# Three FFN down projections: eight of 22 inputs folded into seven block products, in written order

## The chip, the core and the metric

The kernel runs on one core of a Trainium2 chip, as one launch. The metric is device time in microseconds, the median of several runs. The engines are TensorE (PE; its weight loads are PEld), VectorE (DVE), ScalarE (ACT), GpSimd (POOL) and SyncE (SP). SP, ACT and POOL have DMA queues of their own.

## What is computed

An encoder of two layers on 512 tokens of width 1024. Each layer has an FFN, an attention mixer and a second FFN, so there are four FFNs:

```python
def swiglu(h, w_gate, w_up, w_down):
    return (jax.nn.silu(h @ w_gate) * (h @ w_up)) @ w_down
...
        h = rms_norm(x, norm_g[l, 0])
        x = x + 0.5 * swiglu(h, ffn_w_gate[l, 0], ffn_w_up[l, 0], ffn_w_down[l, 0])
```

The inner width is 2816, or 22 blocks of 128; the outer width is 8 blocks of 128. All data is float32. The change touches the last matrix product, `@ w_down`, in the first three FFNs. The fourth has a different ending (`finish`), which also forms the output.

## The kernel before

**Arithmetic.** A float32 factor is written as a high and a low part of type fp32r. A product of two factors is then three matmuls: high by high, high by low, low by high. ScalarE makes a high part by a cast and VectorE the low part by a subtraction. `weights` (L90 to L99) loads a weight tile on SP into `raw`, casts it to `whi` (L96) and subtracts to `wlo` (L97). `parted` (L101 to L106) does the same for a tile that is there already. There are three buffers of `raw` and four each of `whi` and `wlo`, so the fifth cast waits until TensorE is done with the first.

**Tokens** are the moving operand: 512 columns, cut into halves of 256 (`H`) where blocks are formed.

**Gate and up.** A tile `m` (one of the 22 inner blocks) is made by `Seven.tile`. Gate and up weights, with two groups of four inputs, form a 2 x 2 block product which is computed with seven products in place of eight, in the order 1, 5, 6, 2, 7, 3, 4. Sums of weights (`wsum`, `others`) and sums of inputs (`Sides`) are formed beforehand. A product is "joined" (`wide`) where the high and low halves of an input stand side by side as one 512 column operand, so each high weight is used by one matmul of 512 columns in place of two of 256. `Seven.in_order` ties the instructions of a tile on each engine to the order in which they are written; elsewhere a scheduler picks the order. Product 4 of a tile and its gating are put off into the next tile (`self.tail`). At the end of a tile `g`, the gated value, is split into `hi` and `lo`.

**Down.** For each of 8 output blocks, loop over the 22 inputs in chunks of 8, 8 and 6; per input three matmuls of 512 columns (L379, L380 and L382), 66 in an output block, all into one PSUM bank. Then `advance` adds the result to the residual: VectorE scales (L284) and adds (L285); POOL stores the new residual and loads the next (`x_keep`, `x_tile`); ScalarE makes the high part of the next norm's input with its gain (L149) and the square (L160); VectorE makes the low part (L150) and sums the squares (L161). The scheduler orders this stage. The tail of the last gate and up tile (`tiles.flush`) stands behind the first chunk of the first output block.

**Copies for later FFNs.** `ahead_by` issues, in paces, DMAs that form sums of the next FFN's gate and up weights in DRAM (`d_odd`, `d_even`), from ACT's and POOL's queues.

Of the kernel before, what the change touches and what calls it, by code (L numbers as in the profile page):

```python
# [11 lines left out]
F32 = mybir.dt.float32  # L12
# [19 lines left out]
GBUFS = 2 * MF  # L32
# [11 lines left out]
def encoder(ctx: ExitStack, tc: tile.TileContext, a: dict, out: bass.AP):  # L44
# [41 lines left out]
    loaded, lower, kept = [], [], []  # L86
    prepared, ahead, due, owed, queue = {}, [], [], [0.0, 0.0], {}
# [45 lines left out]
    class Norm:  # L133


        def __init__(self, step, gain):
            self.step, self.gain = step, gain
            self.hi, self.lo, self.both = [None] * KC, [None] * KC, [None] * KC
            self.acc = None
# [5 lines left out]
        def parts(self, k, xk):  # L145
            g = self.gain[:, k : k + 1]
            both = self.both[k] = xpool.tile([P, 2, S], F32R, tag=f"h{k}", name=f"h{k}")
            hi, lo = both[:, 0], both[:, 1]
            nc.scalar.activation(hi, xk, AF.Copy, scale=g)  # L149
            nc.vector.scalar_tensor_tensor(out=lo, in0=xk, scalar=g, in1=f(hi), op0=ALU.mult, op1=ALU.subtract)  # L150
            self.hi[k], self.lo[k] = hi, lo

# [53 lines left out]
    def table_loads(fp):  # L206
        nc.gpsimd.memset(tab, 0.0)
        hot.extend(fp.tile([64, 512], F32R, tag="g", name="hot", bufs=GBUFS) for _ in range(2))
        for r in (0, 32):
            nc.gpsimd.dma_start(tab[r : r + 32, 0:8], a["rel_bias_table"][:, 4:12])  # L210
            nc.gpsimd.dma_start(tab[r : r + 32, 32:36], a["rel_bias_table"][:, 0:4])
        for i in range(2):
            nc.gpsimd.dma_start(hot[i], a["one_hot"][:, i * 512 : (i + 1) * 512])

    def position_tables(fp):


        parts = fp.tile([64, 36], F32R, tag="g", name="parts", bufs=GBUFS)
        nc.scalar.copy(parts, tab)
        nc.vector.tensor_tensor(out=parts[32:64], in0=tab[32:64], in1=f(parts[32:64]), op=ALU.subtract)  # L220
        yield
        for i in range(2):
            ps = st_tile()
            nc.tensor.matmul(ps[0:36, :], parts, hot[i], start=True, stop=True)
            td = fp.tile([36, 512], F32, tag="g", name="td", bufs=GBUFS)
# [15 lines left out]
    def small_loads(fp):  # L241
        nc.gpsimd.dma_start(mask, a["na_mask"])
        for l in range(DEPTH):
# [6 lines left out]
            lq = fp.tile([P, 2, 2, 64], F32, tag="g", name="lq", bufs=GBUFS)  # L250
# [5 lines left out]
    def lambda_sums(fp, l):  # L256
        lq = own[l][3]
        lp = fp.tile([P, 2, 64], F32, tag="g", name="lp", bufs=GBUFS)
# [20 lines left out]
    def advance(m, ps, rb, fp, nxt):  # L279

        t = x_tile(m)
        room = quarters(fp)
        d, sq = [room[:, n : n + 2, :].rearrange("p a c -> p (a c)") for n in (0, 2)]
        nc.vector.scalar_tensor_tensor(out=d, in0=ps, scalar=0.5, in1=rb, op0=ALU.mult, op1=ALU.mult)  # L284
        nc.vector.tensor_tensor(out=t, in0=d, in1=t, op=ALU.add)  # L285
        x_keep(m, t, nxt.step)
        nxt.chunk(m, t, lambda: sq)

    def ffn(l, i, h, nxt=None):

        with tc.tile_pool(name="ffn", bufs=1) as fp, ExitStack() as order:
# [77 lines left out]
            for m in range(KC):  # L369
                parts = []  # L370
                for c in range(0, MF, 8):
                    n = min(8, MF - c)
                    parts.append((c, n, cols(weights(a["w_down"][l, i, m, :, c * P : (c + n) * P]), n)))
                ps = mm_tile()
                for c, n, w in parts:
                    if m == 0 and c == 8:
                        tiles.flush()
                    for k in range(n):
                        nc.tensor.matmul(ps, w[k][0], ghi[c + k], start=c + k == 0, stop=False)  # L379
                        nc.tensor.matmul(ps, w[k][0], glo[c + k], start=False, stop=False)  # L380
                    for k in range(n):
                        nc.tensor.matmul(ps, w[k][1], ghi[c + k], start=False, stop=c + k == MF - 1)  # L382
                advance(m, ps, h.rb, fp, nxt)
                if first and m == 1:
                    with tc.issue_after(lower[0]):
                        small_values()
# [5 lines left out]
    def gated(h, fp, pg, pu, ghi, glo):  # L392
        t = quarters(fp).rearrange("p a c -> p (a c)")
        gn, un = t[:, 0:S], t[:, S : 2 * S]
        nc.vector.tensor_tensor(out=gn, in0=pg, in1=h.rb, op=ALU.mult)
        nc.scalar.activation(gn, gn, AF.Silu)
        nc.vector.tensor_tensor(out=un, in0=pu, in1=gn, op=ALU.mult)
        hi, lo = [fp.tile([P, S], F32R, tag="g", name="g", bufs=GBUFS) for _ in range(2)]
# [5 lines left out]
    class Sides:  # L404
# [3 lines left out]
        def __init__(self, fp, h, p, xs):  # L408
            e, o = p, 4 + p
            t = []  # L410
            for k in (e, o):
                x = xs[k]
                if x is None:
                    x = fp.tile([P, S], F32, tag="g", name="xf", bufs=GBUFS)
# [5 lines left out]
            one, other = [fp.tile([P, 2, H], F32, tag="g", name="tsum", bufs=GBUFS) for _ in range(2)]  # L420
# [91 lines left out]

    class Seven:
# [51 lines left out]
        def product(self, n, bank, w, b, start=False, stop=False):  # L565


            (wh, wl), ps, count = w, bank[:, 0], [0]

            def mm(out, wk, bk, last):  # L570
                count[0] += 1
                go, end = start and count[0] == 1, stop and last
                nc.tensor.matmul(out, wk, bk, start=go, stop=end, skip_group_check=True)  # L573

            def high(end):
                for k, bk in enumerate(b):
                    if n in self.wide:
                        mm(bank, wh[k], bk, end and k == 3)
                    else:
                        mm(ps, wh[k], bk[:, 0], False)  # L580
                        mm(ps, wh[k], bk[:, 1], end and k == 3)

            def low(end):
                for k, bk in enumerate(b):
                    mm(ps, wl[k], bk[:, 0], end and k == 3)

            if n in LOW_FIRST:
                low(False)
                high(True)
            else:  # L590
                high(False)
                low(True)
# [11 lines left out]
        def tile(self, m):  # L604
# [94 lines left out]
            hi = fp.tile([P, S], F32R, tag="g", name="g", bufs=GBUFS)  # L699
            lo = fp.tile([P, S], F32R, tag="g", name="g", bufs=GBUFS)  # L700
# [14 lines left out]
            def up():  # L715
# [4 lines left out]
                nc.vector.scalar_tensor_tensor(out=un, in0=un, scalar=-1.0, in1=gn, op0=ALU.mult, op1=ALU.mult)  # L720

            def keep():
                nc.scalar.copy(hi, un)
# [4 lines left out]
    def opening(l, i, h, fp, ghi, glo):  # L728
# [11 lines left out]
        def load(k, queue):  # L740
            xs[k] = fp.tile([P, S], F32, tag="g", name="xf", bufs=GBUFS)
# [55 lines left out]
        for k in range(KC):  # L797
            h.square(k, xs[k], lambda: fp.tile([P, S], F32, tag="g", name="sq", bufs=GBUFS))
# [655 lines left out]
def _lay_out(i):  # L1454
# [5 lines left out]
    o["w_down"] = _tiles(i["ffn_w_down"], MF, KC)  # L1460
# [49 lines left out]
```

## Time and profile before

| | |
|---|---|
| time, median of 3 runs | 2410.55 us (2410.46 to 2410.56) |
| the profiled execution: its own time | 2413.94 us |
| its span, first to last instruction | 2412.2 us |
| mean granted TensorE clock | 0.998 |
| busy: TensorE / VectorE / ScalarE / GpSimd | 2390.6 / 1707.2 / 1333.6 / 363.6 us |
| matmuls | 12762 |

Busy time of TensorE is no measure of work alone: a matmul's row lasts longer than the spacing to the next, since they are pipelined. Spacing is read from the starts in the rows in order of time. A row of VectorE or ScalarE also lasts a little longer than the spacing to the next row where the two do not depend on each other. In rows in order of time, the columns are start, length, engine, line, operation, output and inputs, shape and count; a bracket at the end gives the idle time ahead of the instruction and what ended it. In rows of windows, each engine's busy time is followed by its number of instructions; behind them stand the granted clock, the DMA share and GB/s.

### The profile page before, as it was taken

To read this page: it belongs to the slowest core of one execution; us is meant where nothing else is said; L and a number is where in the kernel's file an instruction comes from. 1 tells how busy PE (TensorE), PEld (TensorE's weight loads), DVE (VectorE), ACT (ScalarE), POOL (GpSimd) and SP (SyncE) were. 2 spreads that over 40 slices of the span, in tenths; PEclk is the share of its full clock that TensorE was granted. 3 is DMA by queue.
4 is the path that set the end of the run, shared out by engine and by line. 5 is a ranking of instruction groups with operands and counts; after the bars stand their busy time and mean duration, and the time that the engine had idled before them with its cause. 6 is when DMAs were issued, how large, how long until landed. Compare 5 with 4: busy or idle time off the path is not lost.

```text
span 2412.2 us, 34903 instructions
## 1 busy us (share of the span) xinstructions
PE 2390.6 (99%) x12762; PEld 2048.6 (85%) x12762; DVE 1707.2 (71%) x3061; ACT 1333.6 (55%) x2435; POOL 363.6 (15%) x524
## 2 busy tenths in 40 slices
PE   9999999999999999999999999999999999999998
PEld 7899888878888888888888888888888888888887
DVE  7999445766766779994389983467666666899832
ACT  6766225755666556663256652267565674566632
POOL 3000014322212110002200001244122100000000
PEclk9999999999999999999999999999999999999999
DMA  6666687687779766759746667765556823455532
GB/s 196 181 182 170 198 252 196 185 221 215 173 193 291 221 184 211 227 195 263 188 175 201 215 211 216 205 176 152 175 150 181 189 95 133 160 190 185 173 119 70
DMA packets 149771, 452.86 MB, mean 188 GB/s; under 512 B 18264, under 2 KB 23688, under 8 KB 148640
## 3 DMA queue, kind: packets, MB, share of 16 engines
q1 hardware_dynamic: 89856, 278.50, 35.0%
q0 software_dynamic: 40352, 107.36, 22.0%
q10 hardware_dynamic: 19392, 64.78, 7.5%
q8 instruction: 100, 1.64, 0.3%
q14 instruction: 71, 0.58, 0.1%
HBM read 428.52 MB, written 138.44 MB: 235 GB/s over the span
## 4 chain that ended last, share of the span: by engine, by line
PE 93%; DVE 4%; ACT 1%; issue 1%; DMA 1%; SPq 0%; POOLq 0%; POOL 0%; ACTq 0%; DVEq 0%
PE mm L573 16%; PE mm L119 8%; PE mm L118 8%; PE mm L121 8%; PE pr L573 8%; PE mm L379 5%; PE mm L380 5%; PE mm L382 5%; PE pv L573 4%; PE mm L1294 2%; PE av L1076 2%; PE mm L1290 2%; PE mm L1289 2%; PE t L1066 1%; DVE wlo L105 1%; PE s L1021 1%
## 5 line engine op out<-in xcount | busy, mean ns | idle before, releaser
L96 ACT CAST whi<-raw 128x1024 fp32r<-128x1024 f32 (+1 forms) x258 | 265.5, 1032 | 399.6 <-PE mm L380 181.7
L97 DVE TENSOR_TENSOR wlo<-raw,whi 128x1024 fp32r<-128x1024 f32 (+1 forms) x258 | 310.0, 1201 | 236.1 <-ACT whi L96 118.9
L118 PE MATMUL mm<-h,whi 128*128 128x512 f32 x800 | 318.2, 398 | 0.0
L119 PE MATMUL mm<-h,whi 128*128 128x512 f32 x800 | 314.0, 392 | 0.0
L379 PE MATMUL mm<-g,whi 128*128 128x512 f32 x528 | 205.4, 389 | 0.0
L380 PE MATMUL mm<-g,whi 128*128 128x512 f32 x528 | 205.4, 389 | 0.0
L121 PE MATMUL mm<-h,wlo 128*128 128x512 f32 x800 | 197.8, 389 | 0.0
L105 DVE TENSOR_TENSOR wlo<-raw,whi 128x1024 fp32r<-128x1024 f32 x156 | 184.2, 1218 | 4.1 <-ACT whi L104 4.1
L121 PEld LDWEIGHTS mm<-h,wlo 128*128 128x128 f32 x800 | 150.1, 188 | 31.4
L119 PEld LDWEIGHTS mm<-h,whi 128*128 128x128 f32 x800 | 150.5, 188 | 28.5
L118 PEld LDWEIGHTS mm<-h,whi 128*128 128x128 f32 x800 | 150.4, 188 | 28.3
L104 ACT CAST whi<-raw 128x1024 fp32r<-128x1024 f32 x156 | 157.0, 1053 | 12.7 <-DMA raw<-in_w_gu 9.6
L382 PE MATMUL mm<-g,wlo 128*128 128x512 f32 x528 | 131.4, 389 | 0.0
L1035 ACT ACTIVATE lg<-lg,negm 128x256 f32<-128x256 f32 (+1 forms) x192 | 114.0, 594 | 29.2 <-DVE negm L1032 28.3
L382 PEld LDWEIGHTS mm<-g,wlo 128*128 128x128 f32 x528 | 99.1, 188 | 20.6
L380 PEld LDWEIGHTS mm<-g,whi 128*128 128x128 f32 x528 | 99.1, 188 | 20.6
L379 PEld LDWEIGHTS mm<-g,whi 128*128 128x128 f32 x528 | 99.1, 188 | 20.6
L705 ACT COPY gu<-mm 128x512 f32<-128x512 f32 (+1 forms) x78 | 42.0, 538 | 124.3 <-PE mm L573 124.3
L476 POOL DMA_DIRECT2D d_odd<-in_w_gu x60 | 51.6, 860 | 378.1 <-DMA d_odd<-in_w_gu 280.7
L626 DVE TENSOR_TENSOR gu<-pr,gu 128x256 f32<-128x256 f32 x234 | 98.1, 419 | 3.8 <-ACT gu L664 1.0
L105 DVE TENSOR_TENSOR wlo<-wsum,whi 128x1024 fp32r<-128x1024 f32 x78 | 94.7, 1214 | 0.0
L104 ACT CAST whi<-wsum 128x1024 fp32r<-128x1024 f32 x78 | 82.1, 1052 | 21.7 <-PE pv L573 21.7
(312 smaller groups left out, 5795.2 us busy)
## 6 DMA issues: line engine op xcount, KB each, us to landing
raw<-in_w_gu SPq DMA_DIRECT2D x94, 512.0 KB, 3.3
d_odd<-in_w_gu ACTq DMA_DIRECT2D x60, 512.0 KB, 6.0
d_even<-in_w_gu ACTq DMA_DIRECT2D x60, 512.0 KB, 6.3
d_odd<-in_w_gu POOLq DMA_DIRECT2D x60, 512.0 KB, 8.0
wsum<-d_odd SPq DMA_DIRECT2D x60, 512.0 KB, 3.3
raw<-d_even SPq DMA_DIRECT2D x60, 512.0 KB, 4.3
raw<-in_w_down SPq DMA_DIRECT2D x48, 512.0 KB, 4.4
raw<-in_w_gate SPq DMA_DIRECT2D x48, 512.0 KB, 6.1
```

The lines of the kernel that those rows point to most:

```text
L96: nc.scalar.copy(hi[:, w], raw[:, w])
L97: lower[:] = [nc.vector.tensor_tensor(out=lo[:, w], in0=raw[:, w], in1=f(hi[:, w]), op=ALU.subtract).ins]
L104: nc.scalar.copy(hi, src)
L105: nc.vector.tensor_tensor(out=lo, in0=src, in1=f(hi), op=ALU.subtract)
L118: nc.tensor.matmul(ps, wh, xhi[k], start=k == 0, stop=False)
L119: nc.tensor.matmul(ps, wh, xlo[k], start=False, stop=False)
L121: nc.tensor.matmul(ps, wl, xhi[k], start=False, stop=k == n - 1)
L379: nc.tensor.matmul(ps, w[k][0], ghi[c + k], start=c + k == 0, stop=False)
L380: nc.tensor.matmul(ps, w[k][0], glo[c + k], start=False, stop=False)
L382: nc.tensor.matmul(ps, w[k][1], ghi[c + k], start=False, stop=c + k == MF - 1)
L573: nc.tensor.matmul(out, wk, bk, start=go, stop=end, skip_group_check=True)
L1035: nc.scalar.activation(p, p, AF.Exp, bias=negm, scale=-1.0, accum_out=total)
```

## The change

Eight of the 22 inputs of a down projection (the first eight) are folded: they form four pairs, and with two output blocks each pair of inputs gives a 2 x 2 block of weights; each token operand is cut into two halves of 256. Four pairs are accumulated, so one "block product" runs over four weight blocks. The other 14 inputs stay plain.

- **Gated values** of the first eight tiles are kept whole in float32 (`whole`, tag `un`), not split. `Folded` forms four differences of each pair on VectorE (t1 to t4) and splits them and the four plain halves into high and low: nine operations on VectorE, five on ScalarE, for each of four pairs.
- **Weights.** `w_down`'s rows are permuted on the host, so that a row tile of eight blocks has the even inputs first. `Operands(j)` loads the two row tiles of outputs 2j and 2j+1 on SP into norm buffers that are free (`h4` to `h7`), and forms four sums on VectorE (`totals`, `more`). Then four splits: `wa` (plain first row), `w31`, `w24` (sums) and `w22` (half of the second row).
- **Stage order.** It starts with the plain part of output blocks 0 to 3, beside which the folds and the first operands are made. Then there are four rounds `j`: seven products for outputs 2j and 2j+1, and then the plain part of block 4+j. Plain sums of blocks are kept in PSUM banks (`plain`) that are otherwise the attention's. Products 2 and 3 are added straight onto the plain bank of block 2j; products 1, 6, 7 and 4 run on in one bank `mm`, from which ScalarE takes a copy after each, and product 5 has a second one. Products 2 and 3 are not joined; 1, 4, 5, 6 and 7 are.
- **All of it stands in `tiles.in_order()`**, so that each of TensorE, VectorE, ScalarE and the queues follows the order in which the code is written. `advance` is split into `advanced` (`begin`: gain and square) and `completed` (low part and sum of squares), which are placed by hand.

The core of the diff (the rest are names, buffer counts and the block product moved out of `Seven`):

```diff
-            for m in range(KC):
-                parts = []
-                for c in range(0, MF, 8):
...
-                advance(m, ps, h.rb, fp, nxt)
+            down(l, i, h, nxt, fp, tiles, ghi, glo)
...
+        def seven(j, w, begin, middle, late):
...
+            product(1, one, blocks(w.wa), side("b11"), start=True)
+            begin()
+            nc.scalar.copy(g[:, 0:2], one)
+            add(q[0], q[0], q[1])
+            product(5, two, blocks(w.w31, S), side(1), start=True, stop=True)
+            nc.scalar.copy(q[4], two[:, 1])
+            add(q[4], two[:, 0], q[4])
+            product(6, one, blocks(w.w24), side(2))
+            nc.scalar.copy(g[:, 1:3], one)
+            add(q[1], q[1], q[2])
+            add(q[1], q[1], q[4])
+            product(2, both[:, 0:1], blocks(w.wa, S), side("b21"))
+            middle()
+            product(7, one, blocks(w.w31), side(3))
+            nc.scalar.copy(g[:, 2:4], one)
+            add(q[2], q[2], q[3])
+            add(q[4], q[4], q[2])
+            product(3, both[:, 1:2], blocks(w.w24, S), side("b22"), stop=True)
+            late()
+            product(4, one, blocks(w22), side(4), stop=True)
...
+            advanced(2 * j)
+            nc.scalar.copy(q[3], one[:, 1])
+            add(q[3], one[:, 0], q[3])
...
+            sum22, gate, fourth, up, keep = tiles.tail
...
+            w8 = split(0, 8, 8)
+            bank(0)
+            plain(0, 8, w8)
+            sum22()
+            gate()
+            w16 = split(0, 16, 6)
+            fourth()
+            w8 = split(1, 8, 8)
+            folds = [Folded(fp, 0)]
+            folds[0].main()
+            up()
+            keep()
+            plain(0, 16, w16)
...
+                def begin():
+                    parts[8] = split(m, 8, 8)
+                    if not last:
+                        coming.totals()
+
+                def middle():
+                    parts[16] = split(m, 16, 6)
+
+                def late():
+                    if not last:
+                        coming.first()
+
+                seven(j, w, begin, middle, late)
+                bank(m)
+                plain(m, 8, parts[8])
...
+                advanced(2 * j + 1)
+                completed(2 * j)
+                coming.second()
+                coming.more()
+                completed(2 * j + 1)
+                plain(m, 16, parts[16])
+                coming.fourth()
+                coming.third()
+                w, coming = coming, Operands(j + 2) if j < KC // 2 - 2 else None
```

How it moves instructions, at two places. First VectorE in the first FFN's down stage, one output block before. `gu` is scratch, `raw`, `whi` and `wlo` are weights:

```order
L284 SCALAR_TENSOR_TENSOR gu<-mm,rb 128x512
L97 TENSOR_TENSOR wlo<-raw,whi 128x1024
L285 TENSOR_TENSOR x<-gu,x 128x512
L150 SCALAR_TENSOR_TENSOR h_2948<-x,ng,h_2948 128x512
L161 TENSOR_TENSOR acc<-acc,gu 128x512
L97 TENSOR_TENSOR wlo<-raw,whi 128x1024
L97 TENSOR_TENSOR wlo<-raw,whi 128x768
```

The same engine now, from the second output of one round to the first add of the next. `rows` are weights to be folded, `wsum` their sums (the first `wlo` is that of w31, the second that of w24, with w22's, `w_3057`, ahead of it), `plain` is a PSUM bank:

```order
L393 TENSOR_TENSOR x<-gu,x 128x512
L167 SCALAR_TENSOR_TENSOR h_3387<-x,ng,h_3387 128x512
L171 TENSOR_TENSOR acc<-acc,sq 128x512
L106 TENSOR_TENSOR wlo<-wsum,whi 128x1024
L393 TENSOR_TENSOR rows<-wsum,rows 128x512
L393 TENSOR_TENSOR rows<-rows 128x512
L167 SCALAR_TENSOR_TENSOR h_3425<-x,ng,h_3425 128x512
L171 TENSOR_TENSOR acc<-acc,sq 128x512
L106 TENSOR_TENSOR w_3057<-rows,w_3056 128x512
L106 TENSOR_TENSOR wlo<-rows,whi 128x1024
L98 TENSOR_TENSOR wlo<-raw,whi 128x1024
L393 TENSOR_TENSOR wsum<-rows 128x512 x2
```

Behind these twelve stands the add of product 1's halves, without which ScalarE may not copy product 6. Before, no add of a product stood in this stage.

Second, ScalarE at the same place, before: two casts of weights, the gain and square of an output, and the next cast.

```order
L96 CAST whi<-raw 128x768
L96 CAST whi<-raw 128x1024
L149 ACTIVATE h_2948<-x,ng 128x512
L160 ACTIVATE gu<-x 128x512
L96 CAST whi<-raw 128x1024
```

And now, from the gain of output 2j to the copy of product 1. L483 copies product 4, L462 product 1; the copies of products 5 and 6 follow:

```order
L158 ACTIVATE h_3387<-x,ng 128x512
L162 ACTIVATE sq<-x 128x512
L483 COPY gu<-mm 128x256
L158 ACTIVATE h_3425<-x,ng 128x512
L162 ACTIVATE sq<-x 128x512
L105 CAST whi<-wsum 128x1024
L105 CAST w_3056<-rows 128x512
L105 CAST whi<-rows 128x1024
L97 CAST whi<-raw 128x1024
L737 DMA d_odd<-in_w_gu 256x1x512
L738 DMA d_even<-in_w_gu 16x8192
L462 COPY gu<-mm 128x512
```

The copy of product 4 stands behind gain and square of the first output, and the copies of products 1, 5 and 6 behind four casts and two DMA issues.

More of the change, by code (lines that the diff above doesn't have):

```diff
@@ L276, in small_values @@
             own[l] = bg, sg, sink, nsink, nlam
[L279 to L287, printed above, removed]
     def ffn(l, i, h, nxt=None):
+        folded[0] = nxt is not None
+        gbufs[0] = 2 * (MF - FOLD) if folded[0] else 2 * MF
+        whole.clear()
         with tc.tile_pool(name="ffn", bufs=1) as fp, ExitStack() as order:
@@ L393, in gated @@
         t = quarters(fp).rearrange("p a c -> p (a c)")
-        gn, un = t[:, 0:S], t[:, S : 2 * S]
+        gn, un, fold = t[:, 0:S], t[:, S : 2 * S], folded[0] and len(ghi) < FOLD
+        if fold:
+            un = whole[len(ghi)] = fp.tile([P, S], F32, tag="un", name="un", bufs=FOLD)
         nc.vector.tensor_tensor(out=gn, in0=pg, in1=h.rb, op=ALU.mult)
         nc.scalar.activation(gn, gn, AF.Silu)
-        nc.vector.tensor_tensor(out=un, in0=pu, in1=gn, op=ALU.mult)
-        hi, lo = [fp.tile([P, S], F32R, tag="g", name="g", bufs=GBUFS) for _ in range(2)]
+        made = nc.vector.tensor_tensor(out=un, in0=pu, in1=gn, op=ALU.mult)
+        if fold:
+            kept.append(made.ins)
+            ghi.append(None)
+            glo.append(None)
+            return
+        hi, lo = [fp.tile([P, S], F32R, tag="g", name="g", bufs=gbufs[0]) for _ in range(2)]
         nc.scalar.copy(hi, un)
@@ L419, in __init__ @@
             b11, b12, b21, b22 = t[0][:, :H], t[0][:, H:], t[1][:, :H], t[1][:, H:]
-            one, other = [fp.tile([P, 2, H], F32, tag="g", name="tsum", bufs=GBUFS) for _ in range(2)]
+            one, other = [fp.tile([P, 2, H], F32, tag="g", name="tsum", bufs=gbufs[0]) for _ in range(2)]
             t1, t2, t3, t4 = one[:, 0], one[:, 1], other[:, 0], other[:, 1]
@@ L511, in drained, with block_product, mm, high @@
                 due.pop(0)
+    def block_product(emit, wide, low_first, n, bank, w, b, start=False, stop=False):
+        (wh, wl), ps, count = w, bank[:, 0], [0]
+        def mm(out, wk, bk, last):
+            count[0] += 1
+            emit(out, wk, bk, start and count[0] == 1, stop and last)
+        def high(end):
+            for k, bk in enumerate(b):
+                if n in wide:
+                    mm(bank, wh[k], bk, end and k == 3)
+                else:
+                    mm(ps, wh[k], bk[:, 0], False)
+                    mm(ps, wh[k], bk[:, 1], end and k == 3)
+        def low(end):
+            for k, bk in enumerate(b):
+                mm(ps, wl[k], bk[:, 0], end and k == 3)
+        if low_first:
+            low(False)
+            high(True)
+        else:
+            high(False)
+            low(True)
     class Seven:
@@ L565, in product, with mm @@
         def product(self, n, bank, w, b, start=False, stop=False):
[L568 to L572, printed above, removed]
+            def mm(out, wk, bk, go, end):
                 nc.tensor.matmul(out, wk, bk, start=go, stop=end, skip_group_check=True)
[L575 to L592, printed above, removed]
+            block_product(mm, self.wide, n in LOW_FIRST, n, bank, w, b, start=start, stop=stop)
         def halves(self, *n):
@@ L698, in tile @@
             u3 = self.halves(1, 6, 7)
-            hi = fp.tile([P, S], F32R, tag="g", name="g", bufs=GBUFS)
-            lo = fp.tile([P, S], F32R, tag="g", name="g", bufs=GBUFS)
+            fold = folded[0] and m < FOLD
+            hi, lo, to = None, None, un
+            if fold:
+                to = whole[m] = fp.tile([P, S], F32, tag="un", name="un", bufs=FOLD)
+            else:
+                hi, lo = [fp.tile([P, S], F32R, tag="g", name="g", bufs=gbufs[0]) for _ in range(2)]
             self.out[0].append(hi)
```

205 lines of the change are left out of this document (179 added, 26 removed).

## The prediction

> **What bounds the kernel now.** I read the page first (busy shares and the chain that ended last), then the stage that the change rewrites, as one window, then its engines in order of time.
>
> ```profile
> PE 2390.6 (99%) x12762; PEld 2048.6 (85%) x12762; DVE 1707.2 (71%) x3061; ACT 1333.6 (55%) x2435; POOL 363.6 (15%) x524
> PE 93%; DVE 4%; ACT 1%; issue 1%; DMA 1%; SPq 0%; POOLq 0%; POOL 0%; ACTq 0%; DVEq 0%
> core 0: us, PE busy (x) PEld busy (x) DVE busy (x) ACT busy (x) POOL busy (x), PEclk, DMA share, GB/s
> 236.70:357.80 121.10, 121.10 (x538) 100.32 (x537) 49.44 (x68) 35.19 (x43) 15.25 (x22) 1.00 0.74 223
> ```
>
> TensorE carries 93% of the chain. In the first FFN's down stage (the window) it never rests, at full clock, while VectorE has 49 us of work in 121 and ScalarE 35. So a saved matmul is worth its full spacing there, as long as the work that now lands on VectorE and ScalarE stays hidden. That second half is what decides.
>
> **What a matmul costs.** These rows are TensorE in order of time: a product with its halves apart, one with them joined, and eight plain matmuls.
>
> ```profile
> 225.31 0.64 PE L573 MATMUL mm<-side,wlo 128*128 128x256 f32 x4
> 225.79 1.12 PE L573 MATMUL mm<-side,whi 128*128 128x256 f32 x8
> 226.75 1.12 PE L573 MATMUL mm<-h,whi 128*128 128x256 f32 x8
> ...
> 228.19 1.09 PE L573 MATMUL pr<-pair,whi 128*128 128x512 f32 x4
> 229.12 0.63 PE L573 MATMUL pr<-pair,wlo 128*128 128x256 f32 x4
> 229.59 0.64 PE L573 MATMUL mm<-h,w22l 128*128 128x256 f32 x4
> ...
> 346.47 1.98 PE L382 MATMUL mm<-g,wlo 128*128 128x512 f32 x8
> 348.28 0.39 PE L379 MATMUL mm<-g,whi 128*128 128x512 f32 x1
> ```
>
> By starts: an unjoined product (12 of 256 columns) takes 226.75 - 225.31 = 1.44 us, a joined one (4 of 512, 4 of 256) 229.59 - 228.19 = 1.40, a plain matmul (348.28 - 346.47) / 8 = 0.226. For two outputs, the eight folded inputs took 2 x 8 x 3 = 48 matmuls, 10.86 us; now they take five joined and two unjoined products, 7.00 + 2.88 = 9.88. That saves 0.98 us per pair of outputs, 3.9 per FFN (four pairs), 11.8 in three. The other 14 inputs cost what they did.
>
> **The start of the stage.** Product 4 of the last gate and up tile stands between the first plain products, and the last of the 22 gated inputs comes out of it. It is now wanted ten matmuls (2.26 us) behind product 4, where before 34 stood in between.
>
> ```profile
> 242.63 1.09 PE L573 MATMUL mm<-h,w22h 128*128 128x512 f32 x4
> 243.56 0.39 PE L379 MATMUL mm<-g,whi 128*128 128x512 f32 x1
> ...
> 243.76 0.37 ACT L717 COPY gu<-mm 128x256 f32<-128x256 f32 x1 [2.16 <-PE mm L573]
> 245.35 0.62 ACT L723 CAST g<-gu 128x512 fp32r<-128x512 f32 x1 [1.22 <-DVE gu L720]
> ...
> 244.16 0.42 DVE L626 TENSOR_TENSOR gu<-mm,gu 128x256 f32<-128x256 f32 x1 [0.53 <-ACT gu L717]
> 244.62 0.69 DVE L720 SCALAR_TENSOR_TENSOR gu<-gu 128x512 f32<-128x512 f32 x1
> 246.00 0.69 DVE L724 TENSOR_TENSOR g<-gu,g 128x512 fp32r<-128x512 f32 x1 [0.69 <-ACT g L723]
> ```
>
> The chain is copy, add, product, cast, low part, with 0.03 to 0.04 from an end to the next engine's start. The high part is ready at 246.01, 2.45 after 243.56: a wait of 0.2. The low part, at 246.73, is wanted one matmul later: 0.5. Together 0.7 per FFN (0.4 to 1.0, since the first fold's VectorE work stands in between).
>
> **What the other engines must now do in a round.** A round is the seven products of one pair of outputs and one plain output block: 9.88 + 42 x 0.226 = 19.4 us of TensorE. Before, 20.4. First prices, VectorE and then ScalarE.
>
> ```profile
> 1302.92 0.88 DVE L626 TENSOR_TENSOR gu<-pr,gu 128x256 f32<-128x256 f32 x2
> 1303.83 0.69 DVE L695 TENSOR_TENSOR gu<-gu,rb 128x512 f32<-128x512 f32 x1
> 1304.44 0.88 DVE L626 TENSOR_TENSOR gu<-gu 128x256 f32<-128x256 f32 x2
> 1305.23 2.35 DVE L105 TENSOR_TENSOR wlo<-raw,whi 128x1024 fp32r<-128x1024 f32 x2
> 1307.50 0.42 DVE L626 TENSOR_TENSOR gu<-pr,gu 128x256 f32<-128x256 f32 x1
> ```
> ```profile
> 271.46 0.75 DVE L150 SCALAR_TENSOR_TENSOR h<-x,ng,h 128x512 fp32r<-128x512 f32 x1 [0.79 <-ACT h L149]
> 272.13 0.68 DVE L161 TENSOR_TENSOR acc<-acc,gu 128x512 f32<-128x512 f32 x1
> ```
> ```profile
> 1313.26 0.59 ACT L705 COPY gu<-mm 128x512 f32<-128x512 f32 x1 [1.74 <-PE mm L573]
> 1313.74 2.00 ACT L104 CAST whi<-raw 128x1024 fp32r<-128x1024 f32 x2
> 1315.64 0.63 ACT L710 ACTIVATE gu<-gu 128x512 f32<-128x512 f32 x1
> ...
> 255.74 0.72 ACT L149 ACTIVATE h<-x,ng 128x512 fp32r<-128x512 f32 x1 [2.72 <-DVE x L285]
> 256.37 0.62 ACT L157 ACTIVATE acc<-x 128x512 f32<-128x512 f32 x1
> 256.95 1.05 ACT L96 CAST whi<-raw 128x1024 fp32r<-128x1024 f32 x1
> ```
>
> Start to start, VectorE: 1024 columns 1.135 (half of 1307.50 - 1305.23), 512 columns 0.61 when the next one needs nothing of it; one that needs its result starts 0.03 after its end (1302.92 + 0.88 to 1303.83), so 0.73 for 512; a low half of h 0.67. ScalarE: copy from PSUM 0.48 for 512 columns (0.59 to its end), 0.37 long for 256, cast of 1024 0.95 (1.05 to its end), gain 0.63, square 0.58.
>
> The stage is in written order, so each engine waits at the head of its queue. Counting one round on VectorE: four low parts of 1024 (4.5), one of 768 (0.9, an estimate between the two sizes), four operand sums and w22's low part (3.2), seven 256 adds of the products (2.8, 0.79 for two above), two outputs of three dependent operations (4.2), two low halves of h and two sums of squares (2.6): 18.2 of 19.4 us. By the sum it fits, barely. By its waits it doesn't. I follow what holds what from product 7 of one round to product 7 of the next, in us from the former's start, with 0.04 for a handover:
>
> - Product 7 ends at 1.56 (0.16 behind its spacing, as 228.19 + 1.09 behind 229.12). ScalarE copies it at 1.60 and casts the next wa at 2.08; VectorE takes its low part at 3.17.
> - VectorE: output 2j at 4.30, 5.03, 5.76, done 6.45. ScalarE then does gain and square *ahead of* the copy of product 4: 6.49, 7.12, copy 7.70 to 8.07. VectorE, idle since 6.45, adds it at 8.11 and does output 2j+1 at 8.57, 9.30, 10.03, done 10.72.
> - ScalarE: gain 10.76, square 11.39, cast of w31 11.97 to 13.02. VectorE waits again: low part 13.06, the two sums of "more" 14.20 and 14.93, low half of h 15.54, squares 16.21, w22 16.82, w24 17.43, the plain part 18.56, the next totals 19.70 and 20.31, and only then q0 at 20.92, done 21.34.
> - ScalarE may overwrite q1 with product 6 only then: 21.38 to 21.97. Product 7 adds onto the same bank: 22.0.
>
> 22.0 against 19.4: TensorE waits 2.6 us in a round. It shows in two places. The cast of w24 waits for "more" (15.66), the plain cast and the copy of product 1 stand behind it (16.61, 17.56 to 18.15), and product 6 needs that bank: 18.2, some 1.6 late. The other 1.0 is product 7. The first round has no such wait, since its operands are made during the four plain blocks ahead of it. The last has no totals (1.22 less), and product 6's wait decides: 18.2 + 1.40 + 1.44 = 21.0. So an FFN waits 2.6 + 2.6 + 1.6 = 6.8 us.
>
> **The rest of the change.** The folds (per pair of inputs nine operations on VectorE, at most 4.4 us, and five casts) lie beside plain blocks of 42 x 0.226 = 9.5 us that need 2 us of VectorE: nothing, and without that cover 4.4 us for each of four. In gate and up, eight of 22 tiles lose a cast (0.62) and a subtraction (0.69):
>
> ```profile
> PE mm L573 <- ACT gu L658: 1.9, 7, 0.5
> PE mm L573 <- DVE wlo L105: 1.6, 4, 0.5
> ```
>
> By these two rows TensorE waits 3.5 us for them in the whole run, for other operations: I take nothing, at most -3.5. The weights' bytes stay, on SP's queue four loads a round as before; the rows to be folded are loaded a round ahead. Two copies for the next FFN that ScalarE issues now stand between the plain cast and the copy of product 1:
>
> ```profile
> 949.57 0.56 ACTq L485 DMA_DIRECT2D d_odd<-in_w_gu  x1
> ```
>
> Two last 1.1 us, 0.2 longer than the cast ahead of them. That shifts product 6, not the loop through q0: nothing, at most 0.2 a round. The residual of output m+2 is loaded when h of output m is done, some 16 us before it is wanted (at 11.3 and 16.2 of the loop above, for 27.8 and 32.0), and lands in:
>
> ```profile
> x<-in_xT POOLq DMA_DIRECT2D x6, 256.0 KB, 7.3
> ```
>
> Hidden with 8 us to spare. **Sum:** per FFN -3.9 + 6.8 + 0.7 = +3.6; three, +10.8. The profiled execution took 2413.94 (span 2412.2) and would take 2424.7; it stands 3.4 over the median of the runs, 2410.55, so I forecast 2421.
>
> **Rivals.** *The loop doesn't bind* (the other side). VectorE's sum fits, and if its handovers overlapped better than I laid out, TensorE would set the pace. It decides at a loop of 20.5 us, where waits and start eat the 3.9; at 19.4 the time is 2410.55 - 11.8 + 2.1 = 2401. Against it: 12% would have to go from a chain of operations that each have a row.
>
> *The waits cost clock.* One wait of this length is in the trace:
>
> ```profile
> 513.64 1.02 PE L1290 MATMUL mm<-yp,whi 128*128 128x512 f32 x2 [2.09 <-DVE yp L130]
> 514.46 3.32 PE L1294 MATMUL mm<-yp,wlo 128*128 128x512 f32 x8
> ...
> 514.00:516.00 2.00, 2.00 (x6) 1.58 (x5) 0.80 (x3) 0.81 (x2) 0.44 (x2) 0.50 1.13 244
> 516.00:518.00 2.00, 2.00 (x7) 1.58 (x7) 0.88 (x2) 0.00 (x0) 0.65 (x2) 0.67 0.99 275
> ```
>
> After 2.09 us without work the granted clock was 0.50, then 0.67, and eight matmuls took 3.32 instead of 1.98. The longest wait of the products before was 0.5. Mine of 1.6 is nearer to 2.09. If it does, products 6 and 2 run slower and product 7 starts 0.7 later, or is itself slow: 0.7 to 1.4 on each of nine loops, 6 to 13 us, so about 2430. [...]
>
> *No overlap on VectorE.* If an operation never started before the one ahead had ended, ten links of the loop would each be 0.08 longer: 22.8, and some 2428 in all. The row against it is 1303.83, 0.69 long, with its successor at 1304.44. [...]
>
> *A late load.* The accumulating loads share POOL's queue with the residual. From 8 us more on it, each round pays the excess: with 1 to 2 us in nine rounds, 2430 to 2439.
>
> **How the numbers follow.** The forecast, 2417 to 2425: 0.54. Clock, drain or late load, 2425 to 2436: 0.23. A loop around 20.0 to 20.8, within 0.2% (4.8 us, about what can be told from no change): 0.13. The saving kept, under 2405.7: 0.10. So slower 0.77. The range, 2412 to 2430, leaves out about one in ten on either side.
>
> **What would show it.** Right: spacing of 1.40 and 1.44 in the products; gaps of about 1.6 ahead of product 6 and 1.0 ahead of product 7 in rounds two and three of each FFN, the first alone in round four, none in round one; VectorE idle twice a round behind ScalarE's square. Wrong: a down stage without gaps (then my chain has a false link), gaps at other places, or a clock under 1 behind them.

## Result, and the profile after

| | before | after |
|---|---|---|
| time, median of 4 runs | 2410.56 us (2410.46 to 2412.12) | 2445.75 us (2443.63 to 2448.21) |
| ratio | | 1.0145, 95% interval 1.0127 to 1.0162 |
| profiled execution / span | 2413.94 / 2412.2 us | 2444.06 / 2442.3 us |

The change costs 35.2 us by the medians, 1.45%; 10.8 were forecast. The page and the waits of TensorE (who waited for whom: us in total, times, longest):

```profile
PE 2388.2 (98%) x12954; PEld 2051.3 (84%) x12954; DVE 1839.1 (75%) x3328; ACT 1380.6 (57%) x2551; POOL 362.0 (15%) x524
PE 84%; DVE 7%; ACT 4%; DMA 3%; issue 2%; ACTq 0%; SPq 0%; POOLq 0%; POOL 0%; DVEq 0%
...
PE mm L390 <- ACT gu L462: 16.4, 10, 2.0
PE plain L390 <- ACT whi L97: 15.1, 2, 11.9
PE mm L390 <- ACT gu L468: 3.6, 6, 0.7
```

L462 and L468 are ScalarE's copies of products 1 and 6: waits ahead of products 6 and 7, which were forecast. The second row was not: plain matmuls waiting for the cast of a plain weight tile, twice, once for 11.9 us. The three stages as windows, before and then after:

```profile
236.69:357.80 121.11, 121.11 (x538) 100.33 (x537) 49.45 (x69) 35.19 (x43) 15.25 (x22) 1.00 0.74 223
1090.08:1211.17 121.09, 121.09 (x537) 100.33 (x536) 50.55 (x63) 35.30 (x43) 25.35 (x34) 1.00 0.80 216
1430.83:1551.92 121.09, 121.09 (x537) 100.32 (x536) 49.43 (x60) 35.39 (x43) 18.56 (x26) 1.00 0.76 223
```
```profile
232.01:358.52 126.51, 120.20 (x602) 101.55 (x601) 97.58 (x164) 60.76 (x96) 15.14 (x22) 0.99 0.68 215
1090.44:1230.83 140.39, 121.41 (x602) 101.61 (x600) 99.16 (x157) 59.16 (x93) 25.11 (x35) 0.95 0.70 198
1449.85:1582.49 132.64, 121.52 (x601) 101.58 (x600) 98.86 (x157) 58.89 (x93) 17.03 (x25) 0.99 0.69 210
```

The first column after the window is its length. The stages got longer by 5.4, 19.3 and 11.6 us, 36.3 in all; outside them the profiled execution is 6.2 shorter (the one of before had lost 3.1 at its very start, where its first gate and up matmul ran at 33.19 us, against 30.11 after). VectorE's work in a stage doubled.

Each stage splits at the first matmul of product 1 into a start (the plain parts of blocks 0 to 3) and four rounds. The rounds of the first FFN, by TensorE's rows in order of time:

```profile
272.33 1.07 PE L390 MATMUL mm<-fold,whi 128*128 128x512 f32 x4
...
291.71 1.07 PE L390 MATMUL mm<-fold,whi 128*128 128x512 f32 x4
...
295.99 1.19 PE L390 MATMUL mm<-pair,whi 128*128 128x512 f32 x4 [1.32 <-ACT gu L462]
...
299.77 0.74 PE L390 MATMUL mm<-side,wlo 128*128 128x256 f32 x4 [0.68 <-ACT gu L468]
...
313.64 1.07 PE L390 MATMUL mm<-fold,whi 128*128 128x512 f32 x4
...
318.63 1.35 PE L390 MATMUL mm<-pair,whi 128*128 128x512 f32 x4 [2.03 <-ACT gu L462]
...
336.83 1.07 PE L390 MATMUL mm<-fold,whi 128*128 128x512 f32 x4
...
341.81 1.20 PE L390 MATMUL mm<-pair,whi 128*128 128x512 f32 x4 [2.02 <-ACT gu L462]
...
358.52 0.39 PE L119 MATMUL mm<-h,whi 128*128 128x512 f32 x1
```

Rounds of 19.38, 21.93, 23.19 and 21.69 us, with the gaps ahead of products 6 and 7. The second FFN's start is where most of the surprise lies; TensorE, then ScalarE in the same stretch:

```profile
1090.44 3.79 PE L390 MATMUL plain<-g,whi 128*128 128x512 f32 x16
...
1123.90 6.05 PE L390 MATMUL plain<-g,whi 128*128 128x512 f32 x16 [11.93 <-ACT whi L97]
...
1145.23 1.07 PE L390 MATMUL mm<-fold,whi 128*128 128x512 f32 x4
```
```profile
1101.17 0.56 ACTq L737 DMA_DIRECT2D d_odd<-in_w_gu  x1
...
1120.29 0.52 ACTq L738 DMA_DIRECT2D d_even<-in_w_gu  x1
1120.85 0.62 ACT L630 CAST right<-un 128x512 fp32r<-128x512 f32 x1 [19.75 <-DMA d_odd<-in_w_gu]
...
1122.81 1.04 ACT L97 CAST whi<-raw 128x1024 fp32r<-128x1024 f32 x1
```

ScalarE's queue stands for 19.75 us at six issues of copies for a later FFN (the rows shown and four between them); the fold of pair 1 and the cast of block 2's weights stand behind. The start lasts 1145.23 - 1090.44 = 54.8 us where its matmuls need 39.5 (168 of 0.226, and product 4). Starts of the three FFNs: 40.3, 54.8, 43.9.

### The profile page after: what moved, and what is told of

Its sections match the earlier page's. It is cut to its first block, busy times and chain, and to the rows that moved or that the text cites. A ratio compares the mean times of both kernels' runs of the same rounds, so it can differ in the third digit from the quotient of the medians.

```text
span 2442.3 us, 35695 instructions
## 1 busy us (share of the span) xinstructions
PE 2388.2 (98%) x12954; PEld 2051.3 (84%) x12954; DVE 1839.1 (75%) x3328; ACT 1380.6 (57%) x2551; POOL 362.0 (15%) x524
## 4 chain that ended last, share of the span: by engine, by line
PE 84%; DVE 7%; ACT 4%; DMA 3%; issue 2%; ACTq 0%; SPq 0%; POOLq 0%; POOL 0%; DVEq 0%
PE mm L848 17%; PE pr L848 9%; PE mm L122 8%; PE mm L119 8%; PE mm L120 8%; PE pv L848 4%; PE plain L390 4%; DMA raw<-in_w_down 2%; PE mm L1558 2%; PE mm L390 2%; PE mm L1554 2%; PE av L1340 2%; PE mm L1553 2%; DVE wlo L106 1%; PE t L1330 1%
## 5 line engine op out<-in xcount | busy, mean ns | idle before, releaser
L98 DVE TENSOR_TENSOR wlo<-raw,whi 128x1024 fp32r<-128x1024 f32 x234 | 280.3, 1199 | 136.8 <-ACT whi L97 117.8
L97 ACT CAST whi<-raw 128x1024 fp32r<-128x1024 f32 x234 | 239.4, 1028 | 244.8 <-PE mm L120 76.9
L106 DVE TENSOR_TENSOR wlo<-raw,whi 128x1024 fp32r<-128x1024 f32 x156 | 184.2, 1218 | 3.9 <-ACT whi L105 3.9
L390 PE MATMUL plain<-g,whi 128*128 128x512 f32 x672 | 164.3, 394 | 16.0 <-ACT whi L97 15.1
L119 PEld LDWEIGHTS mm<-h,whi 128*128 128x128 f32 x800 | 150.4, 188 | 30.4 <-ACT h L158 2.0
L120 PEld LDWEIGHTS mm<-h,whi 128*128 128x128 f32 x800 | 150.5, 188 | 28.5
L390 PEld LDWEIGHTS plain<-g,whi 128*128 128x128 f32 x672 | 127.5, 190 | 45.7 <-ACT whi L97 16.0
L105 ACT CAST whi<-raw 128x1024 fp32r<-128x1024 f32 x156 | 156.8, 1051 | 10.1 <-DMA raw<-in_w_gu 8.7
L106 DVE TENSOR_TENSOR wlo<-wsum,whi 128x1024 fp32r<-128x1024 f32 x90 | 109.6, 1218 | 17.3 <-ACT whi L105 17.0
L105 ACT CAST whi<-wsum 128x1024 fp32r<-128x1024 f32 x90 | 94.6, 1051 | 39.4 <-PE pv L848 32.7
L67 POOL DMA_DIRECT2D x<-d_x x24 | 13.3, 555 | 587.5 <-DVE gu L884 492.4
L1541 DVE TENSOR_TENSOR z<-mm,rb 128x512 f32<-128x512 f32 x48 | 33.2, 691 | 76.3 <-PE mm L122 76.1
L848 PEld LDWEIGHTS mm<-h,whi 128*128 128x128 f32 x624 | 83.7, 189 | 5.6 <-PE st L244 0.4
L848 PE MATMUL mm<-h,whi 128*128 128x256 f32 x624 | 86.9, 281 | 0.0
```

Source lines behind the costliest of these rows:

```text
L97: nc.scalar.copy(hi[:, w], raw[:, w])
L98: lower[:] = [nc.vector.tensor_tensor(out=lo[:, w], in0=raw[:, w], in1=f(hi[:, w]), op=ALU.subtract).ins]
L105: nc.scalar.copy(hi, src)
L106: nc.vector.tensor_tensor(out=lo, in0=src, in1=f(hi), op=ALU.subtract)
L119: nc.tensor.matmul(ps, wh, xhi[k], start=k == 0, stop=False)
L120: nc.tensor.matmul(ps, wh, xlo[k], start=False, stop=False)
```

## Experiments

Two things were to be explained: the starts and the rounds. For the starts the first suspicion was the bunched copies (theory A); the rival was the four loads of weight rows on SP's queue (theory B). For the rounds theory L is the prediction's loop. This table has what the runs gave; each start and round is read from starts of matmuls as above. In the two scheduled versions the first FFN's stage begins inside the last gate and up tile, so its start isn't comparable.

| kernel | starts, FFN 1 / 2 / 3 | rounds, FFN 1 | median us | ratio to before |
|---|---|---|---|---|
| the change | 40.3 / 54.8 / 43.9 | 19.4 21.9 23.2 21.7 | 2445.75 | 1.0145 |
| e1_spread | 40.3 / 53.0 / 42.2 | 19.4 21.9 23.2 21.7 | 2439.35 | 1.0112 (1.0099 to 1.0125) |
| e2_rows | 40.3 / 46.4 / 40.4 | 19.4 21.9 23.2 21.7 | 2435.70 | 1.0097 (1.0084 to 1.0110) |
| e3_loop | 40.3 / 55.0 / 47.1 | 19.4 19.4 19.9 19.9 | 2424.91 | 1.0051 (1.0040 to 1.0062) |
| e4_free | - / 44.7 / 55.8 | 19.4 19.9 19.7 19.4 | 2424.89 | 1.0056 (1.0043 to 1.0069) |
| e5_rows_loop | 40.4 / 45.2 / 40.4 | 19.4 19.4 21.9 19.9 | 2416.71 | 1.0021 (1.0012 to 1.0031) |
| e6_pool_rows | 40.4 / 40.4 / 40.4 | 19.4 21.9 23.2 23.2 | 2425.83 | 1.0059 (1.0046 to 1.0071) |
| e7_fourth | 40.4 / 55.8 / 42.4 | 19.4 20.7 21.3 20.4 | 2430.95, one run | |
| e8_first | 40.3 / 54.8 / 46.0 | 19.4 20.5 21.3 21.3 | 2438.24, one run | |
| e9_pool_loop | 40.4 / 40.4 / 40.4 | 19.4 19.4 19.9 19.9 | 2406.36 | 0.9982 (0.9973 to 0.9991) |
| e10_ending | 40.4 / 40.4 / 40.4 | 19.4 19.4 19.9 19.9 | 2404.06 | 0.9973 (0.9965 to 0.9982) |
| e11_pool_free | - / 39.5 / 39.5 | 19.4 19.9 19.7 19.4 | 2409.54 | 0.9992 (0.9983 to 1.0001) |

The runs come from different chips and times; the median of before beside them was 2410.6 to 2412.2 us, and the ratios are to that.

**e1_spread: the copies.**

```diff
@@ Operands.__init__
-                ahead_by(2 * owed[1])
@@ each round
                 seven(j, w, begin, middle, late)
+                ahead_by(2 * owed[1])
```

> The pairs of copies for a later FFN that the weight rows paid for (two calls in a row at the start of the stage) are now paid one call a round, after product 4; the number of copies is the same. Theory A (ScalarE waits in its own queue for bunched copies to be issued, and the folds and weight casts behind them are late): the start of the stage, 40.3, 54.8 and 43.9 us in the three FFNs, falls to 40.3, about 40.5 and 41 to 44 us; 2445.75 becomes 2425 to 2433. Theory B (the four loads of weight rows, 2 MB ahead of the plain weights on SP's queue, make the plain weights late whatever the copies do): at most 4 us are gained, 2441 to 2446. The rounds keep their 21.9 to 23.2 us under both, or lose up to 0.5 each to the copies that now stand in them.

The start of the second FFN lost 1.8 us of 14.5. The bunch was cut to one pair, and ScalarE was free again at 1108 us, but it then stood for the weights themselves:

```profile
1106.38 0.62 ACT L630 CAST right<-un 128x512 fp32r<-128x512 f32 x1 [5.58 <-DMA d_even<-in_w_gu]
...
1120.08 1.04 ACT L97 CAST whi<-raw 128x1024 fp32r<-128x1024 f32 x1 [11.63 <-DMA raw<-in_w_down]
```

The time, 2439.35, lies in neither theory's range, and nearer to B's. Theory A falls as the main cause: two things were late, and the copies covered the other one.

**e2_rows: the second pair of row loads.**

```diff
@@ Operands.__init__
-                for odd, r in enumerate(self.r):
-                    nc.sync.dma_start(r, ...)
+                if j != 1:
+                    self.load()
@@ the loop over blocks 1 to 3
+                if m == 2:
+                    coming.load()
```

> The second pair of weight-row loads is issued two plain blocks later; the copies stay bunched at the start of the stage. Theory A (bunched copies hold ScalarE's queue): at most 5 us are gained, since ScalarE still stands at six issues in FFN 2; 2440 to 2446. Theory B (the row loads make the plain weights late): 12 to 17 us are gained, 2428 to 2434, and the starts of the second and third FFN's stage fall to about 41 us. A mixture (the issues wait for a transfer ahead of them to land, and the row loads are among those): ScalarE's wait of 19.8 us is halved, 2432 to 2440.

The mixture, at 2435.70: ScalarE's wait at the issues went from 19.8 to 12.1 us, the second start lost 8.4 and the third all of its excess. In the trace of the change, three of the six issues (1108.08, 1111.44 and 1116.79 us) start 0.02 behind the landing of one of the row loads, the last (1120.29) 0.03 behind that of the plain weight load issued at 1094.61, and the first two (1101.17 and 1103.37) 0.02 behind those of earlier copies. By these times the row loads delay both: the plain weights behind them on SP, and through the copies' issues all of ScalarE's queue. What ties an issue on one queue to a landing on another was not shown.

**e6_pool_rows: another queue, the same bytes.**

```diff
-                    nc.sync.dma_start(r, wd[2 * j + odd, :, : FOLD * P])
+                    (nc.gpsimd if j < 2 else nc.sync).dma_start(r, wd[2 * j + odd, :, : FOLD * P])
```

> The first four loads of weight rows go out from POOL's queue in place of SP's, at the same place of the program; bytes, copies and written order are as in the changed kernel. If the plain weights are late because they stand behind 2 MB in SP's own queue: the stall of 11.9 us in FFN 2 falls below 5 and that of 3.2 in FFN 3 goes, 2430 to 2436. If all transfers share engines that are already full (busy share 1.05 there), the queue does not matter: 2441 to 2447.

All three starts are 40.4 us: the stall is gone wholly, more than expected. A window of 30 us in the second FFN's start, of the change and of this kernel (the last three columns are the clock, the DMA share and GB/s):

```profile
1095.00:1125.00 30.00, 17.76 (x76) 13.85 (x75) 11.01 (x23) 6.91 (x14) 5.93 (x8) 0.83 1.06 325
```
```profile
1093.00:1123.00 30.00, 29.69 (x132) 24.13 (x131) 20.42 (x42) 13.40 (x27) 6.43 (x9) 1.00 1.06 338
```

The DMA engines are as busy in both, and TensorE works 17.8 us in one and 29.7 in the other. So the stall is not bandwidth alone; it comes with the place of the row loads. The loads that the plain blocks wait for (issue to landing, from 1085 to 1130 us), of before, of the change and of this kernel:

```profile
raw<-in_w_down SPq DMA_DIRECT2D x8, 512.0 KB, 5.6
```
```profile
rows<-in_w_down SPq DMA_DIRECT2D x4, 512.0 KB, 16.5
raw<-in_w_down SPq DMA_DIRECT2D x3, 512.0 KB, 24.5
```
```profile
rows<-in_w_down POOLq DMA_DIRECT2D x4, 512.0 KB, 12.6
raw<-in_w_down SPq DMA_DIRECT2D x3, 512.0 KB, 11.5
```

In the change, the plain load issued at 1094.61 us, right behind the four row loads, landed 25.7 us later: it was late in the queue and not in its issue. But the order alone doesn't stall. The first FFN issues the same loads in the same order, and its start is 40.3; the row loads from 232 to 272 us (the fifth is a later round's):

```profile
rows<-in_w_down SPq DMA_DIRECT2D x5, 512.0 KB, 4.8
```

POOL's queue, which has the accumulating copies for a later FFN, moved 1.05 MB in these 40 us and 3.90 from 1090 to 1130. So the order in SP's queue seems to cost something only beside that traffic. No run took the traffic away.

By these rows a plain load took 24.5 us to land behind four row loads on the same queue, and 11.5 beside them on another. The rate was nearly the same (325 and 338 GB/s), and the median fell by 19.9 us.

**e3_loop: the rounds.**

```diff
             product(1, one, blocks(w.wa), side("b11"), start=True)
-            begin()
             nc.scalar.copy(g[:, 0:2], one)
             add(q[0], q[0], q[1])
+            begin()
...
-            advanced(2 * j)
             nc.scalar.copy(q[3], one[:, 1])
             add(q[3], one[:, 0], q[3])
+            advanced(2 * j)
```

> Only written order in the rounds is changed: the copy and add of product 4 stand ahead of the output 2j, and the copy and add of product 1 ahead of the plain weights' cast and the next totals. Theory L (the loop of handovers in the prediction): rounds of 19.4 to 20.0 us in place of 21.9 to 23.2, no gap ahead of product 6 or 7, 18 to 24 us less, 2422 to 2428. Rival W (VectorE's amount of work in a round, 17.4 to 18.2 us busy, is the limit, with its small handovers): rounds of 20.8 to 21.5, 2431 to 2437. Rival of late loads: rounds unchanged, 2445.

No work was removed, two pairs of instructions moved, and the time fell by 20.8 us. The four rounds of the first FFN as windows:

```profile
272.53:291.91 19.38, 19.38 (x107) 16.91 (x106) 15.32 (x24) 9.09 (x14) 1.70 (x3) 1.00 0.54 196
291.91:311.29 19.38, 19.38 (x107) 16.91 (x106) 17.09 (x27) 10.25 (x15) 2.87 (x4) 1.00 0.78 253
311.29:331.19 19.90, 19.71 (x108) 16.75 (x107) 17.71 (x28) 10.14 (x15) 5.08 (x8) 1.00 0.74 212
331.19:351.08 19.89, 19.70 (x107) 16.74 (x106) 13.60 (x21) 9.29 (x14) 3.75 (x5) 1.00 0.80 230
```

VectorE is busy 13.6 to 17.7 us in 19.4 to 19.9 and TensorE no longer waits for product copies (the 0.5 left is a 0.2 us wait for a weight's low part, at the spacing by starts). So it was the loop of handovers, and not the amount of work (rival W).

**e7_fourth and e8_first: the two halves of that edit.**

> Only the copy and add of product 4 stand ahead of output 2j; product 1's copy is where it was. By the prediction's loop this takes about 1.0 us out of the loop through VectorE and 0.9 out of the way to product 6: rounds two to four of 20.9 to 21.2 us in place of 21.9 to 23.2, with about 0.6 us ahead of product 6 and 0.9 ahead of product 7. If the position of product 1's copy were all: rounds of 21.9 to 22.6 as before.

> Only the copy and add of product 1 stand ahead of the plain cast and the next totals; product 4's copy is behind gain and square as in the changed kernel. By the prediction's loop: product 6 waits 0.6 to 0.7 us in rounds two and three, product 7 not at all, rounds of 20.0 to 20.2 us. If product 4's place were what sets the loop: rounds of 21 us or more, with the wait moved to another product.

TensorE's waits in the first FFN's rounds, with product 4 moved alone, and with product 1 moved alone:

```profile
299.14 0.74 PE L390 MATMUL mm<-side,wlo 128*128 128x256 f32 x4 [0.66 <-ACT gu L468]
...
316.67 1.20 PE L390 MATMUL mm<-pair,whi 128*128 128x512 f32 x4 [0.72 <-ACT gu L462]
...
320.46 0.74 PE L390 MATMUL mm<-side,wlo 128*128 128x256 f32 x4 [0.69 <-ACT gu L468]
...
338.00 1.20 PE L390 MATMUL mm<-pair,whi 128*128 128x512 f32 x4 [0.73 <-ACT gu L462]
```
```profile
294.94 1.21 PE L390 MATMUL mm<-pair,whi 128*128 128x512 f32 x4 [0.38 <-ACT gu L461]
...
316.27 1.19 PE L390 MATMUL mm<-pair,whi 128*128 128x512 f32 x4 [1.21 <-ACT gu L461]
...
337.60 1.20 PE L390 MATMUL mm<-pair,whi 128*128 128x512 f32 x4 [1.22 <-ACT gu L461]
```

The first came out near the expectation (rounds of 20.9 to 21.2): 20.7 with the gap ahead of product 7 alone, 21.3 with both, 20.4 with the one ahead of product 6 alone, at 0.7 each. The second was expected too small, 0.6 to 0.7 ahead of product 6; with product 4's copy still late the wait is 0.4 in round two and 1.2 in the next two. Neither place is the whole: the rounds are 19.4 to 19.9 with both moved.

**e4_free and e11_pool_free: written order.**

```diff
-        with tiles.in_order():
+        with ExitStack():
```

> The down stage is no longer tied to written order: the scheduler orders it, as it did before the change, and the work is the same. If the positions in the queues cost the time (theories A and L), the scheduler can move copies, product copies and casts past each other: 2400 to 2425. If the work added to VectorE and ScalarE costs it (rival W), order does not matter: 2440 to 2450. If the scheduler places the blocks so that banks or buffers wait, it is above 2450.

At the scheduler's order the rounds are 19.4 to 19.9, without any edit by hand, but the stage still stands at its start in the third FFN:

```profile
PE plain L390 <- ACT g L987: 16.1, 2, 13.9
```

L987 is the last gating's cast, which the scheduler had put behind a weight cast that waited 14.5 us for its load. With the row loads on POOL's queue as well (e11):

> The scheduler orders the down stage, and the first four row loads go out from POOL's queue. If the 13.9 us that the scheduled stage still waited at its start in FFN 3 are the same late plain weights behind row loads on SP's queue: that wait falls below 2 us, rounds stay at 19.4, and the time is 2400 to 2410. If it is the scheduler's own placing of the last gating behind a cast: the wait stays above 8 us and the time is 2416 to 2424.

That wait is gone and the starts are 39.5, as low as the matmuls allow. A wait of 3.5 us for a weight's low part came instead in the second FFN, and the time is not told apart from before.

**e5_rows_loop, e9_pool_loop and e10_ending: both mended.**

> All three edits together: the second pair of row loads two plain blocks later, one pair of copies a round, and the copies of products 4 and 1 ahead of what they stood behind. If stall and loop are separate and nothing else is hidden behind them: starts of 40.3, 40.5 to 41.5 and 40.4 us, rounds of 19.4, 19.4, 19.9 and 19.9, so a stage of 119 to 120 us against 121.1 before the change; with some 2 to 3 us lost at the next stage's first output (a wait of 2.8 us showed there when the rounds were mended), 2403 to 2409 us, faster than before by 2 to 8. If the copies moved into the rounds hold ScalarE there, or the plain weights are late for a third reason: 2410 to 2418.

The three edits together gave 2416.71, in the second range, but not by the copies. The second FFN's plain weights were still 3.1 us late, and in each of the first two FFNs TensorE waited once for L465, here the copy of product 1, 1.2 us. That copy started 0.96 behind the start of the cast ahead of it, as it does in e9's second FFN, where no issue stands between; what was late was the residual's load on POOL's queue, which VectorE adds to output 3:

```profile
309.68 0.69 DVE L393 TENSOR_TENSOR x<-gu,x 128x512 f32<-128x512 f32 x1 [2.02 <-DMA x<-in_xT]
```

In the second FFN VectorE waited 1.56 us for it.

> The first four row loads on POOL's queue and the copies of products 4 and 1 moved ahead, as in the two runs that mended one of them each; the copies for a later FFN stay where the change put them. If the two losses are separate and are all that stood against the saving: starts of 40.35 us, rounds of 19.4, 19.4, 19.9 and 19.9, a stage of 119 us in all three FFNs against 121.1 before the change. From the three stages 6.4 us less than before; 1 to 2 less in gate and up, 2 to 5 more at the first outputs of the next stages, whose operand is late: 2404 to 2410, faster than before by 2 to 8. If the bunched copies come back as waits once the rounds are short: 2412 to 2420.

2406.36, inside the range: faster than before by 0.18% (0.09 to 0.27). The copies stay where the change put them. In the second FFN one round still lost 1.0 to 2.0 us ahead of product 6, in this run and the next: again VectorE waited for the residual's load, 1.04 and 2.01 us.

```diff
                 if last:
-                    completed(2 * j)
                     d, t = outs[m], xs[m]
                     ...
+                    completed(2 * j)
                     plain(m, 16, parts[16])
```

> As the run with both mended, and in the last round the scaled product and its sum for output 7 stand ahead of output 6's low half on VectorE. If VectorE's late finish of the last output (2.8 us of wait in the mixer behind the first FFN) comes from that order: that wait falls to about 1 to 2 us and the time by 1 to 4 us. If it comes from the next stage's weight splits that the scheduler puts between: no change beyond 1 us.

The wait in the mixer fell from 2.75 to 2.29 us, where 1 to 2 were expected; the times, 2404.06 and 2406.36, have overlapping intervals. So this last edit is unclear. The kernel with it is faster than before by 0.27% (0.18 to 0.35).

## Why the prediction was wrong, step by step

- **The matmuls: right.** Without waits the stage needs 39.5 + 4 x 19.38 = 117.0 us; 121.1 before. The saving is 4.1 per FFN where 3.9 was worked out.
- **The start of the stage, by its own term: right; by the rest of the change: the step that failed.** Ten matmuls behind product 4 TensorE waited 0.2 and 0.8 was lost in all, in the first FFN (0.7 forecast). But "The weights' bytes stay, on SP's queue four loads a round as before; the rows to be folded are loaded a round ahead" was true of the bytes of the whole stage (24 loads before and after) and wrong for its parts. A round now has four loads where two outputs had six before, and the start has the rest. There four plain blocks (896 KB each) and four row loads (2 MB) go out over some 40 us, all on SP: about 5.6 MB, where before 40 us had a third of 11.3 MB, 3.7; and the four row loads are issued in a row, ahead of plain weights that are wanted sooner. I asked when the rows were wanted, and not what stood behind them on their queue. I also priced the copies at their issue, 1.1 us a pair, and not at what an issue may wait for (six held ScalarE for 19.75 us). With it fell "nothing" for the folds: their cover was there, but ScalarE was not. Cost: 20.5 us over the matmuls' 39.5 in three starts, where 2.1 were forecast.
- **The rounds: the mechanism right, the size near.** The first round without a wait (19.38, 19.4 forecast), then 21.9, 22.6 and 21.7 (22.0, 22.0, 21.0), where the clock held. The gaps stood ahead of products 6 and 7, and the last round had the first alone. By the brackets they were 1.3 and 0.7 in round two, 2.0 and 0.7 in round three, 2.0 in round four. By starts, which is how 1.6 and 1.0 were worked out, round two lost 1.5 and 0.9. VectorE stood twice behind it, 1.57 and 1.70 us, as the signs said. From product 7 of round two (299.77) the trace follows the chain within 0.15 us up to the end of output 3, 10.72 behind it in both. Then comes a link that it doesn't have, ScalarE's square, which waits until VectorE has summed the square of the output before (in rounds two and three, not in round one, whose first square needs no sum):

```profile
311.85 0.63 ACT L162 ACTIVATE sq<-x 128x512 f32<-128x512 f32 x1 [0.60 <-DVE acc L171]
```

  It stands there six times in the three FFNs, and makes the rounds behind it 0.6 to 0.7 longer than forecast. In three FFNs the rounds lost 28.0 us, 20.4 were forecast. Of the 7.6 between, some 3.9 are this link, 2.1 the clock, and 1.6 a first round in the third FFN whose operands came late from the stalled start.
- **The clock: a rival that came true in part.** Of six waits of 2.0 us, two were followed by a lower clock, 0.50 for 3.41 us. The matmuls behind each took 1.5 us more; in round three of the first FFN the 0.7 ahead of product 7 went with it, so that the round is 0.6 longer. The stretch from product 6 to product 7 in rounds three and four of the first FFN:

```profile
318.63:323.07 4.44, 4.44 (x20) 4.21 (x21) 4.03 (x8) 1.31 (x3) 1.15 (x2) 0.62 1.02 288
341.81:344.75 2.94, 2.94 (x20) 2.75 (x21) 2.57 (x5) 1.09 (x3) 1.85 (x3) 1.00 0.82 166
```

  The same 20 matmuls behind waits of 2.03 and 2.02. The 11.9 us wait cost 2.3 more in the 16 matmuls behind it (5.89 against 3.63 by starts).
- **The late load: the right kind of rival on the wrong queue.** I put it at the residual on POOL's queue, which was never late in this trace; the late ones were on SP's queue. In three mended kernels (e5, e9 and e10) the residual was late too, by 1.0 to 2.0 us.
- **The other rivals.** The loop did bind. "No overlap on VectorE", the "drain" among the chances, fell: no run shows a drain between operations that need nothing of each other, and here too the sum of squares at 316.59, 0.68 long, has its successor at 317.19.
- **Gate and up, taken as nothing and at most -3.5.** The two waits that made up the 3.5 are 1.3 in the trace after (0.8 and 0.5): some 2 us less, a part of the 6.2 outside the stages.

So 36.3 us in the stages are -12.2 (matmuls), +20.5 (starts) and +28.0 (rounds); the forecast had -11.8, +2.1 and +20.4. The starts make up 18.4 of the 25.5 that it missed. What the change could give is seen with both mended: 5 to 7 us.

## What to carry to other kernels

When code goes into written order, follow each DMA queue as an engine of its own: list what is issued between a load and the one behind it, in bytes, and at the stage's edges as well as in its steady state; a load that is wanted late must not stand ahead of one that is wanted soon (24.5 us to land behind the row loads here, 11.5 beside them). Price an issue on a compute engine's queue by what it waits for, not by its length: six of 0.52 to 0.56 us held ScalarE for 19.75 here. And where a bank or buffer goes round between two engines, put the copy that frees it ahead of work that nobody waits for: two such moves were worth 21 us here.

## What the runs showed that was not expected

Full DMA engines did not hurt by themselves: at a share of 1.06 and 325 to 338 GB/s TensorE worked 59% or 99% of the same 30 us, by the queue that the row loads stood in.

In the change the lower clock came in steps of one length. It was granted at 0.50 from 319.51 to 322.92 us and from 1565.37 to 1568.78, 3.41 us each, and the two are 365 such steps apart (1245.86 us, 3.413 a step). Two of the six waits of 2.0 us, each with its step and the next; the first lies wholly in one step, the second across two:

```profile
316.09:319.51 3.42, 1.39 (x7) 0.83 (x6) 3.42 (x5) 2.75 (x4) 2.01 (x3) 1.00 0.76 267
319.51:322.92 3.41, 3.41 (x17) 3.31 (x16) 3.00 (x7) 0.94 (x2) 0.27 (x1) 0.50 0.79 181
```
```profile
339.99:343.40 3.41, 1.59 (x9) 1.40 (x10) 3.41 (x5) 2.04 (x4) 2.87 (x4) 1.00 0.37 91
343.40:346.81 3.41, 3.41 (x27) 3.24 (x26) 2.41 (x5) 1.87 (x3) 0.27 (x1) 1.00 0.99 163
```

So a step with 2.03 us without a matmul (3.42 - 1.39) was followed by half the clock, and one with 1.82 (3.41 - 1.59) was not. Between 60 us and the last 10 us of this trace there are two more stretches at 0.50, on the same grid: from 517.48 to 520.89, one step, and from 1114.81 to 1128.46, four. In the same part of the traces of before and of the change, five steps at full clock had 2.03 to 2.84 us without a matmul, and half the clock followed each of them; the others had at most 1.86, and it followed none. Of the change's six waits of 2.0 us, the two that lie in one step had it behind them, and the four that lie across two had not.

In the change, e1, e2 and e6 together, 14 of 24 such waits had slower matmuls behind them: the first eight of product 2 took 1.51 to 1.92 us by their row, in place of 1.11 or 1.12. A wait of 1.8 us went both ways: at the mixer's first matmuls, eight took 2.74 us behind a wait of 1.83 in e2, and 2.00 behind one of 1.84 in e5.
